# First feed-forward entry on ACT and DVE, and own SBUF tiles for the up weights of one chunk per stage

## The chip, the cores and the metric

The kernel runs on one core of one Trainium2 chip. The time is the device time of one execution, in microseconds (us), and a kernel's time is the median of its runs. TensorE is called PE here, VectorE DVE, ScalarE ACT, GpSimd POOL and SyncE SP; `PEld` in a profile is TensorE's weight load.

## The reference

Two small models run one after the other on a sequence of 256 rows of width 1024. The first is a hybrid attention layer with a mixture of 32 experts. The second has two layers, each with a SwiGLU feed-forward before and behind its mixer, so four feed-forward stages in all, and they are where the change lies:

```python
def swiglu(x, w_gate, w_up, w_down):
    return (jax.nn.silu(x @ w_gate) * (x @ w_up)) @ w_down

def second_block(x, ...):
    h = x                                  # rms_norm of the first model's result
    for layer in range(DEPTH_2):           # 2
        h = h + 0.5 * swiglu(rms_norm_2(h, norm_ffn[layer, 0]), ...)
        hn = rms_norm_2(h, norm_mix[layer])
        h = h + (pool_fox_mixer(hn, ...) if layer % 2 == 0 else mla_mixer(hn, ...))
        h = h + 0.5 * swiglu(rms_norm_2(h, norm_ffn[layer, 1]), ...)
    return rms_norm_2(h, norm_final)
```

The width inside a feed-forward is 2816, and all is float32.

## The kernel before

Every large product is made in three matmuls. A float32 operand is split into a high part H, rounded to the matmul's fp32r type, and the remainder L; the product is H·XH + H·XL + L·XH. `split` (L191 on) does it: ACT writes H (L195, or L199 where a column scale goes in), DVE writes L (L196, L200). The argument `late` puts the L half on another engine. Weights come by DMA from SP's queue into the pool `raw` (6 buffers, L205) and are split into the ring `hl` (8 buffers), in two halves of 128x1024 each (`load_split`, L203).

`ffn(n, g0)` is one feed-forward stage, n = 0 to 3. It walks over 11 chunks of 256 inner columns. A chunk has a gate group (48 matmuls of 128x256 into a PSUM bank `ps`), an up group (48, bank `psq`), and, one chunk later, a down group (48, into four banks `psa`). `project` and `ws` emit them; the first gate group goes by contraction rows instead (`ws_by_k`), so that it can start on the first inputs. Between these groups TensorE's stream holds the small float32 matmuls that make the norm's factor: `add_sums` adds squares over partitions, `rsqrt_of` works out the reciprocal root in small steps (L218 to L224 on DVE, L219 to L229 on POOL), and `row` spreads it over the partitions: it makes two diagonal tiles `dg` (L268 on DVE, L270 on POOL) and multiplies them with a block of ones, two fp32 matmuls (four records in a trace) into `psa` beside or within the second chunk's up group. In the first stage a second `row` follows later (`later`, in the third chunk's `act`).

A list scheduler sets the order on each engine from the program's data dependences; `tc.issue_after(i)` holds what is emitted inside it behind instruction i. Tiles of one pool take turns by tag.

The entry of the first stage follows the last expert pair. `spread` (L984 on, the callables in `due`) multiplies the experts' outputs back into token order, 2 of 8 blocks of `xT` at a time, and DVE adds them into `xT` (L993). The blocks are split into `first_x`, the first stage's input XH and XL, scaled by the columns `gg`. The squares for two sums follow (`squares`, L244 to L253). The first gate weights are split by ACT (H) and by POOL (L, through `late=(G, G)`); the `dg` tiles of the first stage's first `row` are made by POOL too.

The input tiles come from the pool `x8`, the weights from `hl`; both are float32r, 8 KB per partition. In the built program the ring's weights begin at byte 608 modulo 1024 of a partition (96 for their second 128 columns), the input at 32.

At the end, the result goes out in four DMAs, two from ACT's queue and two from SP's (L1527).

Of the kernel before, what the change touches and what calls it, by code (L numbers as in the profile page):

```python
# [10 lines left out]
F32 = mybir.dt.float32  # L11
F32R = mybir.dt.float32r
# [86 lines left out]
def tile_hybrid(ctx: ExitStack, tc: tile.TileContext, d: dict, out: bass.AP, stop=None, dbg=None):  # L99
# [22 lines left out]
    def nm(s):  # L122
        n_names[0] += 1
        return f"{s}_{n_names[0]}"
# [10 lines left out]
    def raw(shape):  # L135
        return raw_p.tile(shape, F32, tag="raw", name=nm("raw"))

    def hl(shape, dt=F32R):
        return hl_p.tile(shape, dt, tag="hl", name=nm("hl"))

    def x8(dt=F32, shape=(128, KD, T)):
        return x8_p.tile(list(shape), dt, tag="x8", name=nm("x8"))
# [48 lines left out]
    def split(src, H, L, scale=None, late=None):  # L191
        if scale is None:
            n = src.shape[1] // 2 if src.shape[1] > 1 and len(src.shape) == 3 and src.shape[1] * src.shape[2] == 2048 else src.shape[1]
            for c in range(0, src.shape[1], n):
                A.activation(H[:, c:c + n], src[:, c:c + n], AF.Copy)  # L195
                (late[c > 0] if late else V).tensor_tensor(L[:, c:c + n], src[:, c:c + n], H[:, c:c + n].bitcast(F32),  # L196
                                                          op=OP.subtract)
        else:
            a = A.activation(H, src, AF.Copy, scale=scale)  # L199
            v = V.scalar_tensor_tensor(L, src, scale, H.bitcast(F32), op0=OP.mult, op1=OP.subtract)  # L200
            return [a.ins, v.ins]

    def load_split(src_ap, shape, late=None):  # L203
        r = raw(shape)
        SP.dma_start(r, src_ap)  # L205
        H, L = hl(shape), hl(shape)
        split(r, H, L, late=late)
        return H, L

# [107 lines left out]
    def pview(a, n):  # L317
        return a.rearrange("p (k f) -> p k f", k=n)
# [197 lines left out]
    po = ps()  # L516
# [469 lines left out]
    def spread(y, GT, b):  # L986
        po = ps()
        for j in (2 * b, 2 * b + 1):
            for n in range(2):
                last = mm(po[:, (j % 2) * T:(j % 2 + 1) * T], y[j // 4][n][:, (j % 4) * 128:(j % 4 + 1) * 128], GT,  # L990
                          n == 0 and j % 2 == 0, n == 1, skip_group_check=True)
        for j in (2 * b, 2 * b + 1):
            V.scalar_tensor_tensor(xT[:, j, :], po[:, (j % 2) * T:(j % 2 + 1) * T], g2c[:, j:j + 1], xT[:, j, :],  # L993
                                   op0=OP.mult, op1=OP.add)
        return last

    pin, due = [], []

    def behind_one(i):
        return tc.issue_after(i) if i is not None else ExitStack()  # L1000
# [47 lines left out]
    for p in range(NEXP // 2):  # L1048
# [13 lines left out]
        if p == 13:  # L1062
            overflow()

    first_x += [x8(F32R), x8(F32R)]
    for b in range(4):
        due.pop(0)()
        for j in (2 * b, 2 * b + 1):
            pins[:] = split(xT[:, j, :], first_x[0][:, j, :], first_x[1][:, j, :], scale=gg[:, j:j + 1])

    pm.close()
    pe.close()
# [61 lines left out]
    def ffn(n, g0, done=None):  # L1134
# [2 lines left out]
        XHL, narrow, *later = prep("nffn", g0) if n else prep_first(pf)  # L1137
        acc4 = []

        def wf(w, c, nk, late=None):  # L1140
            o = (3 * c + w) * 2048
            return load_split(pview(d["wf"][n, :, o:o + 2048], nk), [128, nk, 2048 // nk], late)

        def down(c, aHL, HL):
            first, last = c == 0, c == FC - 1
# [37 lines left out]
        for c in range(FC):  # L1183
            with ExitStack() as es:
                if n + c == 0:
                    for i in pin[-2:]:
                        es.enter_context(tc.issue_after(i))
                if c == 1:
                    es.enter_context(after(pins[1:]))
                HLg = wf(0, c, KD, (G, G) if n + c == 0 else None)  # L1190
                if c == 0:
                    HLu = wf(1, c, KD)
            pg = ps()
            last = project(HLg, pg) if c else ws_by_k(pg, HLg, XHL)
            if c == 1:
                with tc.issue_after(last):
                    r = row(*rn)
                act(*held, r)
            if c:
                with tc.issue_after(shifted[-1] if n else ended[0]) if c == 1 else ExitStack():  # L1200
                    HLu = wf(1, c, KD)
            elif n:
                rn = narrow(last)
            pu = psq()
            last = project(HLu, pu)
            if n + c == 0:
                rn = narrow(last)
            if not c:
                acc4 += [psa() for _ in range(4)]
                held = (c, pg, pu)  # L1210
                continue
            act(c, pg, pu, r)
# [309 lines left out]
    for i in range(2):  # L1522
        A.activation(gained[i], gained[i], AF.Copy, scale=r[:, i:i + 1])
        o = po_.tile([128, 512], F32, name=nm("o"))
        V.scalar_tensor_tensor(o, bank[2 * i + 1], r[:, i:i + 1], nfb[:, 512:], op0=OP.mult, op1=OP.mult)
        for q, (t, E) in enumerate(((gained[i], A), (o, SP))):
            E.dma_start(out[i * 128:(i + 1) * 128, q * 512:(q + 1) * 512], t)  # L1527


def lay_out(i):  # L1530
# [66 lines left out]
```

## Time and profile before

| | us |
|---|---|
| three runs | 1654.90, 1649.27, 1648.03 |
| median | 1649.27 |
| profiled execution, its own time | 1654.91 |
| its span in the trace | 1653.1 |
| first stage, first gate group to last down group | 694.5 to 888 |
| second stage, middle | 1016.8 to 1169 |
| third stage, middle | 1192.8 to 1362.4 |
| fourth stage, middle | 1475.1 to 1636 |

The profile is one execution, recorded by the hardware; its time lies at the upper end of the three runs. A row of a timeline puts neighbouring instructions of one kind together: start, time from the first's start to the last's end, engine, line, operation, output<-inputs, shape, count, and in brackets the idle time before it with what ended it. The chain of waits goes back from the last instruction, at each step to what released it. [...]

### The profile page before, as it was taken

To read this page: it belongs to the slowest core of one execution; us is meant where nothing else is said; L and a number is where in the kernel's file an instruction comes from. 1 tells how busy PE (TensorE), PEld (TensorE's weight loads), DVE (VectorE), ACT (ScalarE), POOL (GpSimd) and SP (SyncE) were. 2 spreads that over 40 slices of the span, in tenths; PEclk is the share of its full clock that TensorE was granted. 3 is DMA by queue.
4 is the path that set the end of the run, shared out by engine and by line. 5 is a ranking of instruction groups with operands and counts; after the bars stand their busy time and mean duration, and the time that the engine had idled before them with its cause. 6 is when DMAs were issued, how large, how long until landed. Compare 5 with 4: busy or idle time off the path is not lost.

```text
span 1653.1 us, 26911 instructions
## 1 busy us (share of the span) xinstructions
PE 1577.7 (95%) x11239; PEld 1248.5 (76%) x11239; DVE 926.0 (56%) x1670; ACT 579.2 (35%) x883; POOL 158.3 (10%) x270
## 2 busy tenths in 40 slices
PE   5988989999999999899999999999999999999997
PEld 2867853344434443499999899999999998899997
DVE  4587545325434423576557557556755567575554
ACT  2444420000000000343444554444544355554342
POOL 0796000000000000110002101000100002010000
PEclk9998999999999999999999999999999999999998
DMA  9763799999999999965555325655555543165520
GB/s 379 312 209 129 258 371 366 412 421 420 421 420 421 421 421 416 388 212 179 184 191 194 103 102 204 204 184 199 182 199 181 182 153 128 64 224 185 181 100 26
DMA packets 62252, 411.11 MB, mean 249 GB/s; under 512 B 6704, under 2 KB 8752, under 8 KB 15920
## 3 DMA queue, kind: packets, MB, share of 16 engines
q1 hardware_dynamic: 61840, 408.85, 65.4%
q8 instruction: 89, 1.46, 0.4%
q10 hardware_dynamic: 288, 0.52, 0.1%
q14 instruction: 35, 0.29, 0.0%
HBM read 408.30 MB, written 1.05 MB: 248 GB/s over the span
## 4 chain that ended last, share of the span: by engine, by line
PE 53%; DVE 4%; DMA 2%; POOL 1%; issue 1%; ACT 0%; DVEq 0%; SPq 0%; ACTq 0%; POOLq 0%
PE psa L149 20%; PE psq L149 16%; PE ps L149 16%; DMA we<-in_we_dram 1%; DVE hl L196 1%; DVE x L200 1%; DMA hl<-in_we_dram 1%; PE psa L459 1%; DVE xT L1155 0%; POOL rt L227 0%; POOL rt L228 0%; POOL ry L219 0%; DVE sq L251 0%; POOL rt L226 0%; POOL ry L229 0%
## 5 line engine op out<-in xcount | busy, mean ns | idle before, releaser
L195 ACT ACTIVATE hl<-raw 128x1024 fp32r<-128x1024 f32 (+1 forms) x338 | 346.9, 1060 | 404.7 <-issue 252.1
L196 DVE TENSOR_TENSOR hl<-raw,hl 128x1024 fp32r<-128x1024 f32 (+1 forms) x336 | 412.2, 1243 | 120.8 <-ACT hl L195 120.5
L149 PE MATMUL ps<-x,hl 128*128 128x256 f32 x3120 | 391.6, 284 | 6.1 <-ACT hl L195 2.7
L149 PEld LDWEIGHTS ps<-x,hl 128*128 128x128 f32 x3120 | 375.1, 190 | 20.8 <-issue 7.2
L149 PE MATMUL psq<-x,hl 128*128 128x256 f32 x2160 | 262.4, 281 | 1.3 <-ACT hl L195 1.3
L149 PEld LDWEIGHTS psq<-x,hl 128*128 128x128 f32 x2160 | 256.9, 190 | 1.5 <-ACT hl L195 1.5
L149 PE MATMUL psa<-aH,hl 128*128 128x256 f32 x1408 | 253.8, 280 | 0.0
L149 PEld LDWEIGHTS psa<-aH,hl 128*128 128x128 f32 x1408 | 217.9, 188 | 0.0
L149 PE MATMUL psa<-aL,hl 128*128 128x256 f32 x704 | 196.9, 280 | 0.1
L149 PEld LDWEIGHTS psa<-aL,hl 128*128 128x128 f32 x704 | 133.6, 190 | 0.4 <-DVE aL L196 0.3
L149 PE MATMUL psa<-hl,XT 128*64 128x512 f32 x464 | 120.8, 599 | 1.4 <-DMA hl<-in_we_dram 1.4
L1040 ACT ACTIVATE ym<-psa,gs 128x512 fp32r<-128x512 f32 x32 | 21.9, 687 | 248.6 <-PE psa L149 243.7
L149 PE MATMUL psa<-raw,XT 128*64 128x512 f32 x368 | 100.4, 598 | 1.4 <-DVEq L862 1.1
L993 DVE SCALAR_TENSOR_TENSOR xT<-ps,mod,xT 128x256 f32<-128x256 f32 x128 | 55.7, 479 | 77.8 <-PE ps L149 77.6
L149 PEld LDWEIGHTS psa<-hl,XT 128*64 128x64 f32 x464 | 34.8, 136 | 55.0 <-issue 46.7
L1164 DVE TENSOR_TENSOR gr<-ps,row 128x512 f32<-128x512 f32 x44 | 30.4, 690 | 80.3 <-PE ps L149 80.3
L1041 DVE SCALAR_TENSOR_TENSOR ym<-psa,gs,ym 128x512 fp32r<-128x512 f32 x32 | 24.0, 750 | 88.1 <-ACT ym L1040 86.4
L149 PEld LDWEIGHTS ps<-GT,ym 128*128 128x128 f32 x256 | 34.2, 188 | 50.2 <-issue 36.6
L1166 DVE TENSOR_TENSOR ur<-psq,row 128x512 f32<-128x512 f32 x44 | 30.4, 691 | 71.2 <-PE psq L149 71.2
L1018 ACT ACTIVATE ac<-psa 128x512 f32<-128x512 f32 x16 | 9.6, 597 | 166.5 <-PE psa L149 140.4
L149 PE MATMUL psa<-hl,aT 128*64 128x512 f32 x240 | 63.4, 615 | 0.3 <-DVE aT L1030 0.2
L1022 DVE TENSOR_TENSOR ac<-ac,psa 128x256 f32<-128x256 f32 x32 | 12.1, 417 | 91.2 <-PE psa L149 91.2
(363 smaller groups left out, 1751.1 us busy)
## 6 DMA issues: line engine op xcount, KB each, us to landing
raw<-in_wf_dram SPq DMA_DIRECT2D x132, 1024.0 KB, 4.9
hl<-in_we_dram SPq DMA_DIRECT2D x88, 1024.0 KB, 18.3
raw<-in_we_dram SPq DMA_DIRECT2D x68, 1024.0 KB, 19.8
raw<-in_ada_dram SPq DMA_DIRECT2D x24, 1024.0 KB, 7.8
we<-in_we_dram SPq DMA_DIRECT2D x23, 1024.0 KB, 18.4
wmw<-in_we_dram SPq DMA_DIRECT2D x11, 1024.0 KB, 17.7
raw<-in_w_in_dram SPq DMA_DIRECT2D x10, 1024.0 KB, 7.3
raw<-in_ab_in_dram SPq DMA_DIRECT2D x8, 1024.0 KB, 4.9
```

Of the source, the lines that this page charges most:

```text
L149: return getattr(PE.matmul(o, l, r, start=start, stop=stop, **kw), "ins", None)
L195: A.activation(H[:, c:c + n], src[:, c:c + n], AF.Copy)
L196: (late[c > 0] if late else V).tensor_tensor(L[:, c:c + n], src[:, c:c + n], H[:, c:c + n].bitcast(F32), op=OP.subtract)
L200: v = V.scalar_tensor_tensor(L, src, scale, H.bitcast(F32), op0=OP.mult, op1=OP.subtract)
L459: PE.transpose(bk[:, n * 128:(n + 1) * 128], P[:, n * 128:(n + 1) * 128], ident)
L993: V.scalar_tensor_tensor(xT[:, j, :], po[:, (j % 2) * T:(j % 2 + 1) * T], g2c[:, j:j + 1], xT[:, j, :], op0=OP.mult, op1=OP.add)
L1018: A.activation(ac, p1, AF.Silu)
L1022: V.tensor_tensor(ac[:, c], ac[:, c], p3[:, c], op=OP.mult)
L1040: last = A.activation(H, py[n], AF.Copy, scale=gs).ins
L1041: V.scalar_tensor_tensor(L, py[n], gs, H.bitcast(F32), op0=OP.mult, op1=OP.subtract)
L1164: V.tensor_tensor(gr, v2(pg), b2(r), op=OP.mult)
L1166: V.tensor_tensor(ur, v2(pu), b2(r), op=OP.mult)
```

## The change

It has three parts. First, the first gate weights are loaded ahead, in the loop that ends the experts, and split there by ACT and DVE alone, one half between each of the first two pairs of sums and the `x` splits that follow; the order of sums, weight halves and `x` splits is written out by `issue_after`. The first `row` makes its `dg` tiles on DVE. Second, the up weights of the second chunk of every stage, and of the fourth chunk of the first stage, go into two tiles of their own, `zH` and `zL`, in the stage's pool `wf`, instead of the ring `hl`. In the built program `zH` and `zL` begin at 32 modulo 1024 (544 for the second 128 columns), so at the place of the input. Third, the four output DMAs all go out from SP's queue.

```diff
-    def load_split(src_ap, shape, late=None):
+    def load_split(src_ap, shape, late=None, own=None):
         r = raw(shape)
         SP.dma_start(r, src_ap)
-        H, L = hl(shape), hl(shape)
+        H, L = own or (hl(shape), hl(shape))
         split(r, H, L, late=late)
         return H, L
...
-            V.scalar_tensor_tensor(xT[:, j, :], po[:, (j % 2) * T:(j % 2 + 1) * T], g2c[:, j:j + 1], xT[:, j, :],
-                                   op0=OP.mult, op1=OP.add)
+            summed[:] = [V.scalar_tensor_tensor(xT[:, j, :], po[:, (j % 2) * T:(j % 2 + 1) * T], g2c[:, j:j + 1], xT[:, j, :],
+                                                op0=OP.mult, op1=OP.add).ins]
...
     first_x += [x8(F32R), x8(F32R)]
+    r = raw([128, KD, 256])
+    SP.dma_start(r, pview(d["wf"][0, :, :2048], KD))
+    first_w = hl([128, KD, 256]), hl([128, KD, 256])
+    done = None
     for b in range(4):
-        due.pop(0)()
+        with behind_one(done):
+            due.pop(0)()
+        done = summed[0]
+        if b < 2:
+            c = slice(4 * b, 4 * b + 4)
+            with tc.issue_after(pin[-1]):
+                A.activation(first_w[0][:, c], r[:, c], AF.Copy)
+            with tc.issue_after(done):
+                done = V.tensor_tensor(first_w[1][:, c], r[:, c], first_w[0][:, c].bitcast(F32), op=OP.subtract).ins
         for j in (2 * b, 2 * b + 1):
-            pins[:] = split(xT[:, j, :], first_x[0][:, j, :], first_x[1][:, j, :], scale=gg[:, j:j + 1])
+            with tc.issue_after(done):
+                pins[:] = split(xT[:, j, :], first_x[0][:, j, :], first_x[1][:, j, :], scale=gg[:, j:j + 1])
+            done = pins[1]
...
+        def own(c):
+
+            if c == 1 or not n and c == 3:
+                return [pf.tile([128, KD, 256], F32R, tag=t, name=nm(t), bufs=1) for t in ("zH", "zL")]
...
                 if n + c == 0:
-                    for i in pin[-2:]:
-                        es.enter_context(tc.issue_after(i))
+                    es.enter_context(after(pins))
...
-                HLg = wf(0, c, KD, (G, G) if n + c == 0 else None)
+                HLg = wf(0, c, KD) if n + c else first_w
...
-                    r = row(*rn)
+                    r = row(*rn, eng=None if n else V)
...
-                    HLu = wf(1, c, KD)
+                    HLu = wf(1, c, KD, own(c))
...
-        for q, (t, E) in enumerate(((gained[i], A), (o, SP))):
-            E.dma_start(out[i * 128:(i + 1) * 128, q * 512:(q + 1) * 512], t)
+        for q, t in enumerate((gained[i], o)):
+            SP.dma_start(out[i * 128:(i + 1) * 128, q * 512:(q + 1) * 512], t)
```

**DVE at the end of the experts.** What follows the last expert's L1041, before; `x_961` and `x_962` are the first input's H and L, `ps_...` the banks of the sums:

```order
L993 SCALAR_TENSOR_TENSOR xT<-ps_5084,mod,xT 128x256 x2
L993 SCALAR_TENSOR_TENSOR xT<-ps_5095,mod,xT 128x256 x2
L200 SCALAR_TENSOR_TENSOR x_962_5083<-xT,gg,x_961_5082 128x256 x4
L993 SCALAR_TENSOR_TENSOR xT<-ps_5106,mod,xT 128x256 x2
L993 SCALAR_TENSOR_TENSOR xT<-ps_5117,mod,xT 128x256 x2
```

And with the change (`hl_5087` is the first gate weights' L, `sq_5250` the running squares):

```order
L993 SCALAR_TENSOR_TENSOR xT<-ps_5088,mod,xT 128x256 x2
L1080 TENSOR_TENSOR hl_5087<-raw_5084,hl_5086 128x1024
L200 SCALAR_TENSOR_TENSOR x_962_5083<-xT,gg,x_961_5082 128x256 x2
L993 SCALAR_TENSOR_TENSOR xT<-ps_5101,mod,xT 128x256 x2
L1080 TENSOR_TENSOR hl_5087<-raw_5084,hl_5086 128x1024
L200 SCALAR_TENSOR_TENSOR x_962_5083<-xT,gg,x_961_5082 128x256 x2
L993 SCALAR_TENSOR_TENSOR xT<-ps_5114,mod,xT 128x256 x2
L251 TENSOR_TENSOR sq_5250<-sq_5250,sq_5253 128x512
L200 SCALAR_TENSOR_TENSOR x_962_5083<-xT,gg,x_961_5082 128x256 x2
L993 SCALAR_TENSOR_TENSOR xT<-ps_5125,mod,xT 128x256 x2
```

Two weight halves and one addition of squares now stand between the sums.

**ACT at the same place.** Before (`hl_5136` are the first gate weights, `hl_5144` the first up weights):

```order
L195 ACTIVATE hl_5136<-raw_5134 128x1024 x2
L199 ACTIVATE x_961_5082<-xT,gg 128x256 x4
L195 ACTIVATE hl_5144<-raw_5142 128x1024 x2
L199 ACTIVATE x_961_5082<-xT,gg 128x256 x4
L247 ACTIVATE sq_5250<-xT,cols 128x256 x2
```

With the change, from the addition for the second sum (`acc_5266`) on:

```order
L244 ACTIVATE acc_5266<-xT 128x512
L195 ACTIVATE zH_5385<-raw_5387 128x1024
L199 ACTIVATE x_961_5082<-xT,gg 128x256 x2
L247 ACTIVATE sq_5257<-xT,cols 128x256 x2
L195 ACTIVATE zH_5385<-raw_5387 128x1024
L199 ACTIVATE x_961_5082<-xT,gg 128x256 x2
L195 ACTIVATE hl_5144<-raw_5142 128x1024 x2
```

The second chunk's up weights (`zH`) now stand ahead of the last four inputs, and the first up weights behind them.

**DVE ahead of the first stage's first row.** Before, the small steps of `rsqrt_of` follow one another, and `dg` is POOL's:

```order
L1114 SCALAR_TENSOR_TENSOR rv_5249<-rw_5133,rv_5249 128x2
L218 TENSOR_SCALAR ri_5285<-rv_5249 128x2
L218 TENSOR_SCALAR ri_5632<-rw_5133 128x2
L219 TENSOR_SCALAR ry_5286<-ri_5285 128x2
L222 SCALAR_TENSOR_TENSOR rt_5287<-ry_5286 128x2
```

With the change (`hl_5503` and `hl_5511` are the first two down weights, `hl_5568` the third chunk's up weights; four rows at the cut are small steps as before):

```order
L1129 SCALAR_TENSOR_TENSOR rv_5249<-rw_5141,rv_5249 128x2
L196 TENSOR_TENSOR hl_5503<-raw_5500,hl_5502 128x1024
L218 TENSOR_SCALAR ri_5285<-rv_5249 128x2
...
L196 TENSOR_TENSOR hl_5511<-raw_5508,hl_5510 128x1024
L222 SCALAR_TENSOR_TENSOR rt_5287<-ry_5286 128x2
...
L196 TENSOR_TENSOR hl_5568<-raw_5565,hl_5567 128x1024
L224 SCALAR_TENSOR_TENSOR ry_5286<-rt_5287,ry_5286 128x2
...
L196 TENSOR_TENSOR zL_5386<-raw_5387,zH_5385 128x1024
L268 TENSOR_SCALAR dg_5360<-cstt,ry_5286 128x128 x2
```

The small steps stand between weight halves, and `dg` comes behind them and the first half of `zL`. On PE, three matmuls of the up group that reads `zH` and `zL` stand ahead of the two of `row`, where none stood before; the third of them is the first that reads `zL`.

## Rows read from the trace of the kernel before

**Rows 1.** The page's first part: busy us, share of the span, instructions.

```profile
PE 1577.7 (95%) x11239; PEld 1248.5 (76%) x11239; DVE 926.0 (56%) x1670; ACT 579.2 (35%) x883; POOL 158.3 (10%) x270
```

**Rows 2.** Windows, PE's matmuls of L149: us, busy (count), PEclk, DMA share, GB/s.

```profile
741.30:888.00 146.70, 146.70 (x1248) 1.00 0.55 186
1016.80:1169.00 152.20, 152.20 (x1345) 1.00 0.57 193
1192.80:1362.40 169.60, 169.60 (x1442) 1.00 0.54 181
1475.10:1636.00 160.90, 160.90 (x1369) 1.00 0.41 138
```

**Rows 3.** Chain of waits in the first and third stage: start us, us, what.

```profile
735.64 5.88 PE psq L149 x52
741.52 5.66 PE psa L149 x48
...
1181.39 5.44 PE ps L149 x48
...
1186.83 0.47 PE psa L149 x4
1187.30 5.66 PE psq L149 x48
1192.95 5.76 PE psa L149 x48
```

**Rows 4.** Timeline of PE at the first stage's entry, columns as told above.

```profile
694.53 7.33 PE L149 MATMUL ps<-x,hl 128*128 128x256 f32 x48 [2.54 <-DVE xT L993]
...
716.84 0.84 PE L149 MATMUL psa<-dg,cstt 128*128 128x128 f32 x4 [3.10 <-POOL dg L270]
717.43 7.32 PE L149 MATMUL psq<-x,hl 128*128 128x256 f32 x48
724.60 0.62 PE L149 MATMUL psa<-aH,hl 128*128 128x256 f32 x4
```

**Rows 5.** Window behind that wait: us, busy of PE, PEld, DVE, ACT, POOL, PEclk, DMA, GB/s.

```profile
719.00:721.00 2.00, 2.00 (x11) 2.00 (x11) 2.00 (x5) 0.63 (x1) 0.52 (x1) 0.50 0.23 90
```

**Rows 6.** Timeline of PE in the experts, a gather.

```profile
617.86 2.14 PE L149 MATMUL ps<-Gt,x 128*128 128x256 f32 x16
```

**Rows 7.** Timeline of POOL at the entry.

```profile
687.74 4.87 POOL L196 TENSOR_TENSOR hl<-raw,hl 128x1024 fp32r<-128x1024 f32 x2 [487.46 <-PE ps L149]
```

**Rows 8.** Timeline of DVE at the entry.

```profile
687.42 1.65 DVE L993 SCALAR_TENSOR_TENSOR xT<-ps,mod,xT 128x256 f32<-128x256 f32 x4
689.04 4.65 DVE L200 SCALAR_TENSOR_TENSOR x<-xT,gg,x 128x256 fp32r<-128x256 f32 x4
...
695.18 1.66 DVE L200 SCALAR_TENSOR_TENSOR x<-xT,gg,x 128x256 fp32r<-128x256 f32 x4
...
700.43 1.22 DVE L196 TENSOR_TENSOR hl<-raw,hl 128x1024 fp32r<-128x1024 f32 x1
...
702.17 0.69 DVE L251 TENSOR_TENSOR acc<-acc,sq 128x512 f32<-128x512 f32 x1
...
712.22 0.16 DVE L224 SCALAR_TENSOR_TENSOR ry<-rt,ry 128x2 f32<-128x2 f32 x1
```

**Rows 9.** Groups by line and shape, DVE's `dg`: busy us, mean ns, idle before.

```profile
L268 DVE TENSOR_SCALAR dg<-cstt,ry 128x128 f32<-128x128 f32 x8 | 2.4, 338 | 0.1
```

**Rows 10.** Timeline of SP's queue: the fourth and fifth weight load of the stage.

```profile
680.65 0.82 SPq L205 DMA_DIRECT2D raw<-in_wf_dram  x2
```

**Rows 11.** DMA issues of 681.0 to 681.5: count, size, median us to landing.

```profile
raw<-in_wf_dram SPq DMA_DIRECT2D x1, 1024.0 KB, 13.7
```

**Rows 12.** Timeline of ACT at the entry.

```profile
686.62 1.99 ACT L195 ACTIVATE hl<-raw 128x1024 fp32r<-128x1024 f32 x2
688.51 1.70 ACT L199 ACTIVATE x<-xT,gg 128x256 fp32r<-128x256 f32 x4
```

**Rows 13.** Timeline of SP's queue at the end.

```profile
1647.77 0.94 SPq L1527 DMA_DIRECT2D out_dram<-o  x2
```

More of the change, by code (lines that the diff above doesn't have):

```diff
@@ L992, in spread @@
         for j in (2 * b, 2 * b + 1):
-            V.scalar_tensor_tensor(xT[:, j, :], po[:, (j % 2) * T:(j % 2 + 1) * T], g2c[:, j:j + 1], xT[:, j, :],
-                                   op0=OP.mult, op1=OP.add)
+            summed[:] = [V.scalar_tensor_tensor(xT[:, j, :], po[:, (j % 2) * T:(j % 2 + 1) * T], g2c[:, j:j + 1], xT[:, j, :],
+                                                op0=OP.mult, op1=OP.add).ins]
         return last
-    pin, due = [], []
+    pin, due, summed = [], [], []
     def behind_one(i):
@@ L1138, in ffn, with wf @@
         acc4 = []
-        def wf(w, c, nk, late=None):
+        def wf(w, c, nk, own=None):
             o = (3 * c + w) * 2048
-            return load_split(pview(d["wf"][n, :, o:o + 2048], nk), [128, nk, 2048 // nk], late)
+            return load_split(pview(d["wf"][n, :, o:o + 2048], nk), [128, nk, 2048 // nk], None, own)
+        def own(c):
+            if c == 1 or not n and c == 3:
+                return [pf.tile([128, KD, 256], F32R, tag=t, name=nm(t), bufs=1) for t in ("zH", "zL")]
         def down(c, aHL, HL):
```

## The prediction

> **What bounds the kernel now.** First the page: PE is busy 95% of the span and no other engine comes near it [rows 1]. So I read how fast TensorE's stream runs, stage by stage, before any wait. Over the long middle of each of the four feed-forward stages PE is busy all the time, at granted clock 1.00, and still the stages differ: 146.70 us for 1248 matmuls in the first, 152.20 for 1345 in the second, 169.60 for 1442 in the third, 160.90 for 1369 in the fourth [rows 2]. That is 117.5, 113.2, 117.6 and 117.5 ns each, for the same shape, the same order and the same clock. The chain says it plainer, since nearly all of it is groups of 48 matmuls: a group takes 5.44 us or 5.65, and a stage stays with one of the two [rows 3]. I call them the quick and the slow pace; a group differs by 0.21.
>
> The next thing to see is where the pace turns. The third stage begins quick (48 in 5.44 at 1181.4). Then come the four records of the small fp32 matmuls that `row` puts into the stream, and from the next group on it is slow, 5.66, 5.76, then 5.65 to its end. The first stage turns in the same place: 5.88 for 52 that include the second `row`, then 5.66. The second is quick after its `row`, the fourth slow [rows 2, 3]. So an interruption can leave either pace, and a stage keeps what it got. That is all the trace shows; it doesn't show what makes a pace.
>
> Last, the entry of the first stage, 685 to 741 us. Here PE does wait: the first gate group of 48 begins at 694.53 and takes 7.33, the second chunk's up group begins at 717.43 behind the `row` records of 716.84 and takes 7.32, and the down group follows at 724.60 [rows 4]. [...]
>
> **Part one: the placement.** In the built programs the weights (`hl`) begin at 608 and, for the second 128 columns, at 96 modulo 1024 bytes of a partition; the input begins at 32. For five groups (one per stage, two in the first) the new tiles put the weights at 32 and 544. Each of the five is the first or third group behind a `row`. Work doesn't change: same matmuls, and the splits of these weights go the same way over ACT and DVE. What it can change is the pace of these five groups and, because a pace lasts, that of the rest of the stage.
>
> The trace of before has no fp32r matmul with weights and input at the same place. Nearest are the quick and slow group (5.44, 5.76 at most in a stretch without a wait [rows 3]); further off is the gather of the experts, with weights at 32 and 544 and moving rows at 352, 16 in 2.14 us, which makes 6.4 for 48 [rows 6]. So the five groups cost between -1.0 (as much below the quick pace as the slow one is above it; no row is below 5.44) and +4.8. I take 5.65, the nearest: +1.0.
>
> What they leave behind decides the case. 48 matmuls under another address relation are a far longer disturbance than the four records that turn the pace now, and the same one in every stage, so I expect the same result in each: all quick or all slow. I take quick as the likelier, because the quick pace is what the trace shows directly after most waits (at 1181.39 [rows 3], and through the whole second stage). Then the first stage gains 23 groups (741 to 888 is 26; two run before the fourth chunk's up group, and that is the third), the third stage 30 (1192.95 to 1362.4), the fourth 28 (1475 to 1636): 81 x 0.21 = -17.2 us. The second is quick already.
>
> **Part two: the entry without GpSimd.** Gone: GpSimd's split of the first gate weights (4.87 for two halves), beside which four `x` splits on DVE took 4.65 instead of 1.66 [rows 7, 8]. That is 3.0 us on the path to 694.53. But the order puts other work there. On DVE now: two sums into `xT` (0.41 each), a weight half (1.2), two `x` splits (0.41 each) [rows 8], again all that, then the third pair of sums, which frees the PSUM bank of the first gate group. From 687.42: 0.82 + 1.2 + 0.82, twice, + 0.82 = 693.9. So the start gains 0.6, not 3.0.
>
> Then ACT. The first half of the new `zH` stands ahead of the inputs 4 to 7. It is the fifth weight load, the second of two issued from 680.65 on, at 681.1; one issued there takes 13.7 to land, so it is there at 694.8 [rows 10, 11]. ACT then needs zH 1.0, two inputs 0.85, two squares (taken at an input's 0.43 each) 0.85, zH 1.0, two inputs 0.85 [rows 12]: 699.3. DVE's last input is ready at 699.8, the first group ends by 700.8 (now 701.9, 694.53 + 7.33 [rows 4]), and the first up group, whose weights come behind that on ACT and DVE (700.3, 701.5), ends at 706.8. Behind these halves DVE has four additions of squares (0.69), two of half that width (0.4) and two weight halves (1.22) [rows 8], 6.0, and waits for ACT's squares, say 0.6: the second sum of squares ends at 708.1, and the second gate group, whose turn comes behind the small matmuls that read it, runs from there, 44 x 0.115, to 713.5.
>
> DVE's queue is now the path. Between the sums and `dg` stand seven weight halves, the last two being the third chunk's up weights, whose buffer is free when the second gate group ends: 713.5 + 2.1 for two ACT halves + 1.2 = 716.8; DVE's own queue from 708.1 (seven halves of 1.15, eight small steps of 0.16, 0.2 with their issue [rows 8]) comes to 717.6. I take 718.2, both with their latencies. Seven small steps of 0.2 follow, 1.4; the first half of `zL`, 1.2; `dg`, two of 0.34 [rows 9]: 721.4. The third matmul of the second up group reads `zL`, so PE stands from 713.7 to 720.8, and the `row` records follow at 721.4. They end at 722.0; then 45 matmuls at 0.113 and the 1.7 that the lower clock adds to this group now (717.43 to 724.60 is 7.2, for 5.44 [rows 4]), 5.1 + 1.7: 728.8 against 724.60. **The entry costs 4.2 us**, since the wait for GpSimd's `dg` is gone and one for DVE's longer queue is there. From both sides: 1.0 if the gate group starts at the full clock (1.3 less) and the halves are as short as 1.13; 6.0 if ACT and DVE wait on each other once more in each pair.
>
> **Part three: the end.** The four stores go out from one queue instead of two by two from 1647.7 on [rows 13]. A store takes that queue 0.35 to 0.5, so the last is issued 0.5 later: +0.5 (0 to 1).
>
> **The sum.** The profiled execution took 1654.9: -17.2 + 1.0 + 4.2 + 0.5 = -11.5, so 1643.4. The other two runs of before are 5.6 and 6.9 below it, about what one stage at the other pace is worth (30 x 0.21 = 6.3). If that is what they are, quick stages bring all runs to 1643; if the profiled run is merely 6 longer, to 1637. I take the middle, **1640 us**.
>
> **The rivals.**
> Placement does nothing. [...] The trace neither shows nor excludes it: pace changes there come with interruptions, at one placement. In this kernel it would mean that `row` decides as now, and only entry and end count: 1649.3 + 4.7 = 1654.0, within 0.5%.
>
> The five groups leave the slow pace (the other side). Then the second stage loses its 30 groups (+6.3), the first another three (+0.6), and entry, end and the groups' own time cost 5.7: 1654.9 + 12.6 = 1667.5, slower than before. It decides from the point where the group behind the second stage's up group takes 5.65. For it: two of the three groups that follow a `row` directly in stages two to four run slow now. Against it: the second stage, with the same order, doesn't.
>
> Each stage falls as it likes. Half of 111 groups (81 slow now, 30 quick) slow: -81 x 0.105 + 30 x 0.105 = -5.4, + 5.7: about 1650 to 1655, by which run of before one starts from.
>
> **How the numbers follow.** Quick everywhere 0.56, with 1634 to 1647; no effect 0.22 (1650 to 1656); slow everywhere 0.12 (1660 to 1670); mixed 0.10 (1644 to 1656). The range 1634 to 1656 leaves out the slow case and the edges. About 0.5%, 8.2 us, is what a measurement of this kernel can tell from no change, so faster means below 1641.0: some 0.68 of the first case and 0.3 of the mixed one, 0.42. Slower means above 1657.5: the slow case and what is left of the others' upper ends, 0.19. The rest, 0.39, is same.
>
> **What would show it.** In the chain of the changed kernel: 5.44 from the group behind each of the five up groups to the stage's end, and 5.44 to 5.8 for the five themselves. 5.65 in the second stage would be the slow case; a pace that differs between stages, with the turn still at `row`, no effect. In the entry: the second up group's third matmul waits some 7 us for DVE's `zL`, and the first down group starts near 729; if it starts before 724.6, my reading of DVE's queue is wrong. If the five groups take over 6.4 each, my bound for them is.

## The result and the profile after

The changed kernel takes 1676.59 us, the median of four runs from 1676.21 to 1677.48. The kernel before took 1649.98 in the runs beside it (1648.03 to 1654.90). The ratio is 1.0158, interval 1.0127 to 1.0189: slower, by 27 us between the medians. The forecast was 1640 with a range from 1634 to 1656.

The profiled execution took 1676.21 against 1654.91. The first part of its page (busy time, share and instructions of each engine), beside [rows 1], shows PE with the same 11239 matmuls, and busy with them 11 us longer:

```profile
PE 1588.9 (95%) x11239; PEld 1258.1 (75%) x11239; DVE 924.9 (55%) x1674; ACT 578.2 (35%) x883; POOL 161.5 (10%) x266
```

So the first view to read is again the pace by stage. These are windows inside the four stages, matmuls of L149 alone, columns as in [rows 2] (PEclk is the granted clock, as a share of full speed):

```profile
751.50:888.00 136.50, 136.50 (x1160) 1.00 0.53 179
1024.00:1169.00 145.00, 145.00 (x1233) 1.00 0.54 182
1216.00:1362.40 146.40, 146.40 (x1246) 1.00 0.54 181
1508.10:1636.00 127.90, 127.90 (x1088) 1.00 0.45 155
```

That is 117.5 to 117.7 ns a matmul in the four, the slow pace. The second stage, 113.2 in [rows 2], is slow too now. The chain of waits shows where it begins. These are the end of the entry and the second stage's beginning (start us, us, what), to be read beside [rows 3, 4]:

```profile
720.24 0.58 PE psq L149
720.82 0.85 PE psa L149 x4
721.67 6.75 PE psq L149 x45
728.42 5.65 PE psa L149 x48
...
1011.60 0.84 PE psa L149 x4
1012.44 5.75 PE psq L149 x48
1018.20 5.65 PE psa L149 x48
1023.85 5.65 PE ps L149 x48
```

At 1012.44 stands the group whose weights lie at the input's place. It takes 5.75, and everything behind it 5.65.

The second thing to see is the rows that come late. The timeline of POOL has the first small step of each `row`, and the timeline of DVE what runs beside it in the second stage:

```profile
999.94 7.82 POOL L219 TENSOR_SCALAR ry<-ri 128x2 int32<-128x2 int32 x1 [56.38 <-DVE ri L218]
...
1190.50 7.83 POOL L219 TENSOR_SCALAR ry<-ri 128x2 int32<-128x2 int32 x1 [178.60 <-DVE ri L218]
...
1478.18 6.76 POOL L219 TENSOR_SCALAR ry<-ri 128x2 int32<-128x2 int32 x1 [76.52 <-DVE ri L218]
```

```profile
999.60 0.17 DVE L218 TENSOR_SCALAR ri<-rv 128x2 int32<-128x2 int32 x1
999.67 1.23 DVE L196 TENSOR_TENSOR hl<-raw,hl 128x1024 fp32r<-128x1024 f32 x1
1000.80 2.36 DVE L196 TENSOR_TENSOR zL<-raw,zH 128x1024 fp32r<-128x1024 f32 x2
1003.08 4.63 DVE L196 TENSOR_TENSOR hl<-raw,hl 128x1024 fp32r<-128x1024 f32 x4
```

A step on two numbers per partition, 0.20 elsewhere, takes 7.82 and ends at 1007.76. DVE's seven weight halves end at 1007.71. In the kernel before the same step took 3.28 beside three halves (995.26 for 3.50), and it ended at 998.80, where they ended at 998.76. The same two views of the kernel before, in the second stage and then in the third:

```profile
995.52 3.28 POOL L219 TENSOR_SCALAR ry<-ri 128x2 int32<-128x2 int32 x1 [56.37 <-DVE ri L218]
...
995.26 3.50 DVE L196 TENSOR_TENSOR hl<-raw,hl 128x1024 fp32r<-128x1024 f32 x3
...
1178.84 1.03 POOL L219 TENSOR_SCALAR ry<-ri 128x2 int32<-128x2 int32 x1 [174.12 <-DVE ri L218]
...
1178.59 2.36 DVE L196 TENSOR_TENSOR hl<-raw,hl 128x1024 fp32r<-128x1024 f32 x2
```

In the second stage of both kernels POOL's step ends when DVE's unbroken run does, and the run is now four halves longer. The reading is that the ring holds DVE back less, because two of its buffers came free; that the own tiles lengthen the run, e2_entry_only and e3_own_only show below. That the step ends with the run is no rule: in the third stage of before it ended at 1179.87, 0.05 behind the first of two halves (1179.81), and the second followed without a gap. Why POOL got its turn there isn't shown. The timeline of PE shows what the late step costs in the changed kernel:

```profile
1011.60 0.84 PE L149 MATMUL psa<-dg,cstt 128*128 128x128 f32 x4 [1.96 <-POOL dg L270]
...
1202.17 1.15 PE L149 MATMUL psa<-dg,cstt 128*128 128x128 f32 x4 [2.23 <-POOL dg L270]
...
1488.79 1.09 PE L149 MATMUL psa<-dg,cstt 128*128 128x128 f32 x4 [3.10 <-POOL dg L270]
```

Set against the same places of the kernel before, the 21.3 us between the two profiled executions are:

| where | us |
|---|---|
| entry, to the first down group (728.25 in the timeline, for 724.60 [rows 4]; the chain, which sets a start behind the modelled end of the matmul before, has 728.42) | 3.7 |
| first stage: three groups that were quick before (0.6), the fourth chunk's own group (0.1) | 0.7 |
| second stage: row late, slower group behind it | 2.6 |
| second stage's slow pace, up to the third stage's row: 31 groups (6.5), less 0.4 for shorter waits | 6.1 |
| third stage: row late (2.4), lower clock in the group behind (0.52 from 1204 to 1206, 1.00 behind that; 6.94 for 5.66 [rows 3]) and in the row (0.63 from 1202 to 1204) | 4.2 |
| fourth stage: row late (2.8), the same (0.50 from 1490 to 1492; 6.89) | 4.2 |
| end | -0.2 |

The medians lie further apart, 26.6, since the profiled execution of before was one of its slowest, and the runs of the changed kernel all lie within 1.3 us.

### The profile page after: what moved, and what is told of

Read it like the earlier page. It is cut to its first block, busy times and chain, and to the rows that moved or that the text cites. A ratio compares the mean times of both kernels' runs of the same rounds, so it can differ in the third digit from the quotient of the medians.

```text
span 1674.4 us, 26902 instructions
## 1 busy us (share of the span) xinstructions
PE 1588.9 (95%) x11239; PEld 1258.1 (75%) x11239; DVE 924.9 (55%) x1674; ACT 578.2 (35%) x883; POOL 161.5 (10%) x266
## 4 chain that ended last, share of the span: by engine, by line
PE 69%; DMA 15%; POOL 8%; DVE 5%; issue 1%; ACT 1%; SPq 0%; DVEq 0%; POOLq 0%; ACTq 0%
PE psa L149 31%; PE ps L149 20%; PE psq L149 16%; DMA hl<-in_we_dram 6%; DMA raw<-in_we_dram 5%; POOL acc L584 3%; POOL tap L583 3%; DMA we<-in_we_dram 2%; POOL ry L219 1%; DVE hl L196 1%; DMA raw<-in_wf_dram 1%; DMA raw<-in_ada_dram 1%; PE psa L459 1%; ACT x L199 0%; PE psq L1029 0%
## 5 line engine op out<-in xcount | busy, mean ns | idle before, releaser
L195 ACT ACTIVATE hl<-raw 128x1024 fp32r<-128x1024 f32 (+1 forms) x326 | 334.3, 1060 | 405.7 <-issue 243.7
L196 DVE TENSOR_TENSOR hl<-raw,hl 128x1024 fp32r<-128x1024 f32 (+1 forms) x326 | 400.0, 1244 | 126.1 <-ACT hl L195 125.9
L149 PE MATMUL ps<-x,hl 128*128 128x256 f32 x3120 | 393.0, 284 | 5.0 <-ACT hl L195 2.7
L149 PEld LDWEIGHTS ps<-x,hl 128*128 128x128 f32 x3120 | 376.6, 190 | 19.7 <-issue 7.2
L149 PE MATMUL psa<-aH,hl 128*128 128x256 f32 x1408 | 256.2, 281 | 0.0
L149 PE MATMUL psq<-x,hl 128*128 128x256 f32 x1920 | 233.6, 281 | 0.3 <-DVE hl L196 0.3
L149 PEld LDWEIGHTS psq<-x,hl 128*128 128x128 f32 x1920 | 228.9, 189 | 0.5 <-DVE hl L196 0.5
L149 PEld LDWEIGHTS psa<-aH,hl 128*128 128x128 f32 x1408 | 220.3, 190 | 0.0
L149 PE MATMUL psa<-aL,hl 128*128 128x256 f32 x704 | 197.5, 281 | 0.0
L149 PEld LDWEIGHTS psa<-aL,hl 128*128 128x128 f32 x704 | 132.2, 188 | 0.0
L219 POOL TENSOR_SCALAR ry<-ri 128x2 int32<-128x2 int32 (+1 forms) x7 | 23.8, 3393 | 1024.3 <-DVE rt L223 518.3
L149 PE MATMUL psa<-hl,XT 128*64 128x512 f32 x464 | 120.4, 599 | 0.3 <-DMA hl<-in_we_dram 0.3
L149 PE MATMUL psa<-raw,XT 128*64 128x512 f32 x368 | 101.9, 607 | 1.4 <-DVEq L862 1.1
L149 PEld LDWEIGHTS psa<-hl,XT 128*64 128x64 f32 x464 | 35.0, 136 | 53.3 <-issue 46.5
L149 PEld LDWEIGHTS ps<-GT,ym 128*128 128x128 f32 x256 | 34.5, 190 | 52.2 <-issue 39.1
L1041 DVE SCALAR_TENSOR_TENSOR ym<-psa,gs,ym 128x512 fp32r<-128x512 f32 x32 | 24.0, 751 | 86.6 <-ACT ym L1040 84.9
L149 PEld LDWEIGHTS psa<-raw,XT 128*64 128x64 f32 x368 | 29.4, 139 | 47.3 <-issue 41.2
```

Source lines behind the costliest of these rows:

```text
L149: return getattr(PE.matmul(o, l, r, start=start, stop=stop, **kw), "ins", None)
L219: E.tensor_scalar(y.bitcast(I32), iv, -1.0, 1597463007.0, op0=OP.mult, op1=OP.add)
L1041: V.scalar_tensor_tensor(L, py[n], gs, H.bitcast(F32), op0=OP.mult, op1=OP.subtract)
```

## The experiments

Three theories stood at the start. The **queue theory**: the extra buffers let DVE run ahead, and the late rows and the entry's loss come from that. The **place theory**: a group's distance between weights and input sets the pace that the stage then keeps, and distance 0 leaves the slow one. The **chance theory**: a pace falls anew at each interruption, and the place has nothing to do with it. "Distance" is weights minus input modulo 512 bytes, so that both 128-column halves of a group have the same; the ring's is 64.

To compare paces across kernels, matmuls are counted in the same four stretches of each profiled execution (770 to 870, 1040 to 1150, 1220 to 1330, 1500 to 1600 us), one in each stage. Quick is 885, 973, 973, 885; slow is 852, 937, 937, 852.

| kernel | 1st | 2nd | 3rd | 4th | median us | ratio to before (interval) |
|---|---|---|---|---|---|---|
| before | 852 | 973 | 937 | 852 | 1649.98 | |
| changed | 851 | 936 | 937 | 851 | 1676.59 | 1.0158 (1.0127 to 1.0189) |
| e1_own_ring_place | 851 | 973 | 936 | 885 | 1663.03 | 1.0054 (1.0024 to 1.0083) |
| e2_entry_only | 851 | 973 | 937 | 885 | 1643.46 | 0.9951 (0.9928 to 0.9974) |
| e3_own_only | 851 | 973 | 936 | 851 | 1678.60 | 1.0181 (1.0141 to 1.0222) |
| e5_hold | 852 | 973 | 973 | 885 | 1654.99 | 0.9995 (0.9972 to 1.0018) |
| e6_own128 | 885 | 973 | 973 | 885 | 1656.25 | 1.0035 (1.0006 to 1.0064) |
| b1_reset128 | 885 | 973 | 973 | 884 | 1637.57 | 0.9909 (0.9877 to 0.9942) |
| b1_same_chip | 885 | 973 | 973 | 885 | 1637.26 | 0.9889 (0.9872 to 0.9907) |
| b4_reset0 | 852 | 937 | 936 | 851 | 1656.32 | 1.0021 (1.0001 to 1.0042) |
| b2_ring320 | 851 | 973 | 936 | 852 | 1650.89 | 0.9967 (0.9950 to 0.9983) |
| b3_ring448 | 852 | 936 | 936 | 852 | 1660.93 | 1.0024 (1.0011 to 1.0038) |

The kernel before was measured beside each group of runs, on several chips: 1651.69 (19 runs, 1642.9 to 1661.6) beside e1 to e3, 1656.38 (23 runs) beside b1_reset128, b2, b3 and e5, 1653.58 (18 runs) beside b1_same_chip, b4 and e6. Its runs spread over 20 us. By an estimate from the traces, 26 to 31 groups a stage at 0.21, four stages that can each be 6 us slower or not give about that.

### The parts apart

**Without tiles of their own** (all up weights in the ring, the rest as changed):

```diff
-                    HLu = wf(1, c, KD, own(c))
+                    HLu = wf(1, c, KD)
```

> The changed kernel without tiles of their own: all up weights lie in the ring again, the new entry and the stores from one queue stay. Queue theory: DVE's small steps stand together again and dg comes behind one weight half, POOL L219 takes 3.5 us or less in the second and third stage, no wait for the row is there; the first down group starts at 718 to 721, 4 to 7 us earlier than before. Rival (the new entry itself costs the 3.8 us): first down group at 727 or later. Time by the queue theory with paces as before 1644 to 1651, by the rival 1653 to 1660.

The entry falls within the queue theory's range, and the time, 1643.46, just below the 1644 to 1651 that it gave. The chain of waits there:

```profile
713.62 0.35 PE psq L149 x3
713.98 0.45 PE psa L149 x4
714.42 5.30 PE psq L149 x45
719.72 0.23 PE ps L149 x2
719.96 2.11 PE psa L149 x17
```

The `row` follows the up group's third matmul without a wait, and the down group starts at 719.96 in the chain and 719.79 in the timeline, 4.8 us earlier than before and 8.5 earlier than in the changed kernel. POOL's step is back at 3.28 in the second stage. So the new entry by itself is a gain, and the 3.7 us that it lost in the changed kernel belong to the own tiles, whose weight halves stood between DVE's small steps and `dg`.

**Only the own tiles**, on the kernel before, old entry:

```diff
-                    HLu = wf(1, c, KD)
+                    HLu = wf(1, c, KD, own=own(c))
```

> The kernel before with one difference: the tiles of their own, at the input's place, for the second chunk's up weights of each stage and the fourth's of the first. Queue theory: POOL L219 takes 7 to 8 us in the second, third and fourth stage, and some 10 us are lost to rows that come late; in the entry dg is POOL's and comes behind DVE's longer queue too. Placement theory: all stages at 5.65 behind these groups. Both together 1668 to 1676. If the new entry was what made POOL's step long, it takes 3.3 us at most here and the time is below 1660.

POOL's step in the second stage is as long as in the changed kernel, with the old entry around it:

```profile
1001.33 7.82 POOL L219 TENSOR_SCALAR ry<-ri 128x2 int32<-128x2 int32 x1 [56.28 <-DVE ri L218]
```

The time, 1678.6, lies 2.6 us above the range that was expected. Another thing was not expected: the profiled execution (1672.04, the quickest of its four runs) has the second stage quick (973), although a group at distance 0 stands there. Its chain of waits there, with that group at 1013.86:

```profile
1013.02 0.84 PE psa L149 x4
1013.86 7.26 PE psq L149 x48
1021.12 5.44 PE psa L149 x48
```

The group stands behind a late row. Its first pairs of matmuls took 0.60 to 0.63 and its later ones 0.40, as in the third stage of the changed kernel, where pairs of 0.63 stand at granted clock 0.52 and pairs of 0.40 at 1.00; so I take it to have begun at the lower clock. It took 7.26, and no wait lies between it and the quick group behind it. In the changed kernel the groups of the third and fourth stage began at the lower clock as well (0.52 and 0.50; 6.94 and 6.89) and left the slow pace. So a group that the clock's rise falls into doesn't always leave the same pace; the undisturbed one at 1012.44 in the changed kernel left the slow one.

**The own tiles at the ring's place** (a pad of 576 bytes ahead of them, 608 modulo 1024):

```diff
+                pf.tile([128, 144], F32, tag="zpad", name=nm("zpad"), bufs=1)
                 return [pf.tile([128, KD, 256], F32R, tag=t, name=nm(t), bufs=1) for t in ("zH", "zL")]
```

> The changed kernel with one difference: the tiles of their own lie at 608 modulo 1024, the place of the ring's weights, and no longer at the input's. Queue theory (two more buffers let DVE run six or seven weight halves without a break, and POOL's first small step of the row waits for the end of that run): nothing changes in it, POOL L219 again takes 7 to 8 us in the second, third and fourth stage, and the row is late there by some 2, 4 and 4 us; the entry is as in the changed kernel, first down group at 728.4. Placement theory (the groups at the input's place leave the slow pace): the five groups then run like any other, and at least the second stage goes back to 5.44 us a group, -6.3 us: about 1670. Chance theory (a stage's pace falls anew at every interruption, whatever the place): stages differ from one execution to another, and the runs spread over 6 us or more below 1677.

POOL's L219 takes 7.82, 7.83 and 6.76, and the first down group starts at 728.2: the queue's part is untouched. The paces are mixed again, two quick stages in the profile, and the runs spread from 1652 to 1665, below all runs of the changed kernel. The median is 1663.0, where the place theory gave some 1670 for the second stage alone; in the profile the fourth is quick too. So buffers and place are two separate losses. The spread is what the chance theory expected as well; what speaks against that one comes below.

**DVE's run cut short.** In the second to fourth stage two of DVE's loads make their L halves only behind the copy of the row (L273):

```diff
+                held_by[:] = copied if n and not c else []
                 prev.append((c, (aH, aL), wf(2, c, 2)))
+                held_by[:] = []
...
+                held_by[:] = copied if n and c == 2 else []
                 HLg = wf(0, c, KD) if n + c else first_w
+                held_by[:] = []
```

> The changed kernel with one difference: in the second to fourth stage DVE makes the L halves of the first chunk's down weights and of the third chunk's gate weights only behind the copy of the row. Queue theory: two halves instead of seven stand ahead of POOL's first small step, L219 takes 2 to 3 us, the row of the second and third stage is in time again and that of the fourth comes 4 to 5 us earlier; the stages stay slow behind the groups at the input's place: 1676.6 - 2.1 - 2.4 - 4.9, about 1667. If POOL's wait has another cause, L219 stays at 7 to 8 us and the time at 1676.

The small step is short (L224 is this kernel's L219):

```profile
997.18 1.02 POOL L224 TENSOR_SCALAR ry<-ri 128x2 int32<-128x2 int32 x1 [55.38 <-DVE ri L223]
```

It takes 1.02 in the second and the third stage, 1.09 in the fourth, and the rows of all three stages come without a wait for `dg`. So a shorter run of DVE does make the rows timely, as forecast. Two sizes are not as forecast. The step takes 1.02 where 2 to 3 were expected. And the time is 22 us less than the changed kernel's, where 9.4 were expected, on a chip where the kernel before was 6 slower. The held halves make PE wait 0.2 us for `aL` just behind the group at distance 0, and the stage turns quick there; the third and the fourth stage have the same wait (0.22 and 0.21) and turn in the same place. That is the profiled execution, the quickest of ten; the others took up to 1663.28 and have no trace. The timeline of PE has the wait, the chain what follows:

```profile
1015.27 0.38 PE L149 MATMUL psa<-aL,hl 128*128 128x256 f32 x1 [0.22 <-DVE aL L201]
```

```profile
1020.52 5.21 PE ps L149 x46
1025.74 5.44 PE psq L149 x48
```

So this run settles the cause of the late rows, but its time mixes two effects.

### What sets the pace

**Eleven distances in one kernel.** On the kernel before, the up weights of the chunks 3, 5, 7 and 9 go into a tile of their own, each time at another distance. No `row` and no wait stands beside these groups. It ran once, in 1646.55 us:

```diff
+        PROBE = ({3: 0, 5: 128, 7: 256, 9: 384}, {3: 0, 5: 192, 7: 320, 9: 448},
+                 {3: 32, 5: 96, 7: 224, 9: 64}, {3: 0, 5: 128, 7: 256, 9: 384})
...
-                    HLu = wf(1, c, KD)
+                    HLu = wf(1, c, KD, own=own(c))
```

> The kernel before with a tile of its own for the up weights of the chunks 3, 5, 7 and 9 of every stage, each time at another distance from the input modulo 512 bytes (first and fourth stage 0, 128, 256, 384; second 0, 192, 320, 448; third 32, 96, 224 and 64, which is the ring's own distance). These groups stand between other groups, with no interruption beside them. Placement theory: a group at distance 0 takes 5.75, and what follows it is slow (5.65) even where the stage was quick; another distance may leave 5.44. Chance theory: the stage goes on at the pace that it had, whatever the place; only the groups themselves differ.

The chain of the second stage, from a quick stretch over a group at distance 0 (1035.86) to one at 192 (1069.89) and one at 320 (1102.74):

```profile
1030.42 5.44 PE ps L149 x48
1035.86 5.76 PE psq L149 x48
1041.62 5.65 PE psa L149 x48
...
1069.89 5.65 PE psq L149 x48
1075.54 5.44 PE psa L149 x48
...
1102.74 5.44 PE psq L149 x48
1108.18 5.44 PE psa L149 x48
```

All sixteen groups:

| distance | the group itself, us | pace ahead to pace behind |
|---|---|---|
| 0 | 5.76 | slow to slow, quick to slow twice |
| 256 | 5.76 | quick to slow twice |
| 128 | 5.70 | slow to quick twice |
| 384 | 5.70 | slow to quick twice |
| 192 | 5.65 | slow to quick |
| 32, 96, 224 | 5.68, 5.76, 5.60 | quick to quick |
| 64, 320, 448 | 5.44 | quick to quick |

The chance theory falls for undisturbed groups: the pace turns right at these groups, at no interruption, and each distance that came more than once did the same each time. The place theory holds, with the sign against the forecast: distance 0, which the change chose, leaves the slow pace. What a stage gets at a `row` or behind a wait is not settled by this run.

**One group per stage, 128 against 0.** On the kernel of e2_entry_only the fourth chunk's up weights of every stage get their own tile, at distance 128 (b1) or 0 (b4). The two kernels differ by one offset:

```diff
+            if c == 3:
+                z = pf.tile([128, 4128], F32R, tag="z", name=nm("z"), bufs=1)
+                return [z[:, o:o + 2048].rearrange("p (k c) -> p k c", c=256) for o in (32, 2080)]   # b1
+                                                                                 for o in (0, 2048)]    # b4
```

> The kernel of e2_entry_only with one difference: the fourth chunk's up weights of every stage lie in a tile of their own, 128 bytes from the input's place modulo 512 (160 and 672 modulo 1024). Place theory (what a group with another distance leaves behind, the stage keeps; p1 showed 128 leave the quick pace twice where the stage was slow): every stage is at 5.44 from the fourth chunk's down group on, whatever it was ahead; two slow stages of e2 gain 22 groups of 0.21 each, the reset group costs 0.05 to 0.26: about 1635, and the runs lie closer together than those of e2. Chance theory: 1643 and paces as they fall. Queue theory: the tile stands behind the row and costs nothing there, POOL L219 as in e2.

> The kernel of b1_reset128 once more, on the chip of b4_reset0, so that the two differ by the distance of one group per stage alone. Place theory: every stage at 5.44 from the fourth chunk's down group on, 1635 to 1638. Chance theory: as b4_reset0.

> The kernel of b1_reset128 with one difference: the fourth chunk's tile lies at the input's place modulo 512 (distance 0), no longer 128 bytes from it. Place theory: a group at distance 0 leaves 5.65 behind it, so all four stages are slow from the fourth chunk's down group on: 88 groups of 0.21 more, 18 us, so about 1655. Chance theory: no difference from b1.

In both, the second stage came to that group slow. The chain of b1_same_chip, then of b4_reset0:

```profile
1025.73 5.66 PE ps L149 x48
1031.39 5.70 PE psq L149 x48
1037.09 5.45 PE psa L149 x48
```

```profile
1028.60 5.65 PE ps L149 x48
1034.26 5.76 PE psq L149 x48
1040.02 5.65 PE psa L149 x48
```

All four stages quick with 128, all four slow with 0, on the same chip 1637.26 against 1656.32: 19.1 us, where 18 were expected. b1 is also the quickest kernel of this study, 1.1 per cent below the kernel before and 0.9 per cent in its first measurement. Its first four runs were 1635.0 to 1637.9 with one at 1646.7, which has no trace; why it was longer is open.

**The changed kernel with its tiles moved by 128 bytes:**

```diff
+                pf.tile([128, 32], F32, tag="zpad", name=nm("zpad"), bufs=1)
                 return [pf.tile([128, KD, 256], F32R, tag=t, name=nm(t), bufs=1) for t in ("zH", "zL")]
```

> The changed kernel with one difference: its own tiles lie 128 bytes further on, at 160 and 672 modulo 1024. Place theory: the five groups then leave the quick pace; stages one to four at 5.44 unless a wait or a second row behind the group throws the pace anew: 70 to 105 groups of 0.21 less, 1655 to 1662. Queue theory: L219 still takes 7 to 8 us and the first down group still starts near 728, since the tiles are as many as before. Chance theory: spread as in e1_own_ring_place, around 1663.

The windows of its four stages:

```profile
770.00:870.00 100.00, 100.00 (x885) 1.00 0.56 192
1040.00:1150.00 110.00, 110.00 (x973) 1.00 0.57 192
1220.00:1330.00 110.00, 110.00 (x973) 1.00 0.57 193
1500.00:1600.00 100.00, 100.00 (x885) 1.00 0.53 179
```

All are quick, POOL's step is as long as ever (7.83 in the second stage), and the entry's stop for `zL` is there too:

```profile
719.65 0.58 PE L149 MATMUL psq<-x,zL 128*128 128x256 f32 x1 [5.48 <-DVE zL L196]
```

The median is 1656.25, 20 us below the changed kernel. Its runs spread over 17 us, 1650.7 to 1668.0. Its groups stand behind late rows, as those of e3_own_only do, so probably not every execution gets the pace that an undisturbed group would leave; only one execution has a trace, so this isn't shown. This is the nearest thing to undoing the place alone, and it shows both halves: by the medians the place cost some 20 us, and with it mended the own tiles still leave the kernel no quicker than before. The other half has a size too: b1_same_chip, on the same chip, is quick in all four stages as well, has its own tile in the fourth chunk only, and its profiled execution is 15.0 us shorter (1638.98 against 1654.00).

**The whole ring at another distance.** The gap between ring and input is made 256 or 384 bytes smaller, on e2_entry_only:

```diff
-    gap(448)
+    gap(192)    # b2: distance 320
+    gap(64)     # b3: distance 448
```

> The kernel of e2_entry_only with the gap between ring and input 256 bytes smaller: every group of every stage, gate, up and down, has its weights 320 bytes from the input modulo 512 and no longer 64. In p1 a group at 320 in a quick stage took 5.44. If the distance decides which paces there are, and 320 has the quick one alone: all four stages at 5.44 throughout, about 1632. If 320 has a slow pace of its own too: stages differ again, 1638 to 1655. The same by chance theory.

> As b2_ring320, with the gap 384 bytes smaller than in e2_entry_only, which makes the distance 448 modulo 512. In p1 a group at 448 in a quick stage took 5.44. Quick pace alone: about 1632; a slow pace of its own: 1638 to 1655.

No gain: with 320 both paces occur, as with 64 (one quick stage of four in the profile), with 448 all four stages are slow, and the median, 1660.93, lies above the 1638 to 1655 expected. So a distance that left a quick stage quick, once, is not one that has the quick pace alone. A single group in an undisturbed stretch turned slow stages quick, at 128 in p1_places and b1_same_chip (5.70 itself, 5.46 and 5.45 behind it) and at 192 and 384 in p1_places; the whole ring at 128 was not run.

## Why the prediction was wrong

**What bounds the kernel.** The reading held: two paces, 5.44 and 5.65, kept by a stage, and TensorE's stream as the path.

**The entry** was worked out as 4.2 and measured 3.7. Its steps came within 0.6 us: first gate group 693.9 (694.22), the stop for `zL` to 720.8 (720.24), `dg` 721.4 (720.82 in the chain), first down group 728.8 (728.25 in the timeline). The experiment adds what the sum didn't say: without the own tiles this entry gains 4.8, so all of its loss comes with the halves that the own tiles let in, PE's stop behind them (5.61) and the lower clock behind the stop. That clock was 0.50 from 720 to 724 in the changed kernel, as it was from 719 to 721 in the kernel before [rows 5]; the 45 matmuls behind the `row` took 6.75, where 5.1 and 1.7 were summed.

**The five groups themselves**: +1.0 was taken, 5.65 each; undisturbed ones took 5.75, which against the slow pace that they had before is 0.1 each.

**The step that failed** is "I take quick as the likelier". That the same result would stand in every stage was right; which one was put on a pace seen behind waits, not on any group at that distance. The term of -17.2 (81 groups at 0.21 are 17.0) became +6.7 (second stage's pace 6.1, three groups of the first 0.6). The trace of before had no such group, and with the sign unknown the honest weight was nearer even than 0.56 to 0.12. The rival "the five groups leave the slow pace" named the mechanism and its price, 1667.5 from the profiled execution of before; that of the changed kernel took 1676.2.

**The missing term** is 11.0 us: second to fourth stage, rows that come late and slower groups right behind them. The sum put it at nothing. "The splits of these weights go the same way over ACT and DVE" is true of the work and not of the times. I costed the longer queue of DVE at the entry and did not look at the other three stages, where DVE now makes 7, 7 and 6 weight halves between its last small step (L218) and the row's copy, for 5, 4 and 4 before, and where the trace of before showed POOL's step in the second stage ending 0.04 us behind DVE's run. The trace of the changed kernel has 7.82 us for a step that takes 0.20 alone: it ended 0.05 behind the last of seven DVE instructions in a row, while in the third stage of before it took 1.03 and ended behind the first of two. What holds POOL's step meanwhile isn't shown.

**The end**: +0.5 was taken, about 0.2 was there from the last DVE instruction to the span's end (5.6 against 5.4); the table's -0.2 holds 0.4 that the last steps ahead of it took less.

**Placement does nothing** falls as well: entered at the quick pace in p1_places, groups take 5.44 to 5.76 by the distance alone, at granted clock 1.00. Why the distance counts isn't shown.

What stays open is what a pace is inside TensorE, which pace a `row` leaves, why a wait of 0.2 us behind a group at distance 0 was followed by the quick pace (e5_hold), and what a group leaves when the clock rises within it (e3_own_only against the changed kernel). The runs show what turns an undisturbed stretch, not how.

## What to carry to other kernels

Where a stream of equal matmuls has more than one pace, find out what turns it by moving one group inside an undisturbed stretch, and read the group behind it; then place one such group per stretch, away from waits. A buffer that is added is a change of order on the engine that fills it: list what that engine now runs ahead of each small step that another engine waits for, in every stage and not only in the one that was edited. And where single runs spread by as much as one stage's pace, one profiled execution is one throw: compare medians of many.

## What the runs showed of the hardware

- fp32r matmuls of 128x256 ran at 113.3 or 117.7 ns each over whole groups of 48 (5.44 or 5.65 us) and at 113.3 to 120 in the sixteen groups of p1_places (5.44 to 5.76), all at granted clock 1.00, by the distance in SBUF between weights and moving rows and by what ran ahead. At one distance (64) both paces persist: in the kernel before 113.2 ns over 152.20 us and 117.6 over 169.60 [rows 2].
- In b1_same_chip the second stage came slow (5.66) to one group of 48 at distance 128, which took 5.70, and left it quick (5.44); all four stages are quick in their windows (885, 973, 973, 885). With that group at 0, in b4_reset0, the second stage came slow and stayed so (5.65, the group 5.76, then 5.65), and all four are slow (852, 937, 936, 851). In p1_places a group at 0 that was entered at 5.44 took 5.76 and left 5.65 behind it.
- Beside seven back-to-back weight halves on DVE (8.0 us) a GpSimd instruction on 128x2 numbers took 7.82 us in the changed kernel and ended 0.05 us behind them; in e5_hold, which holds part of these halves back, it took 1.02. In the third stage of the kernel before such an instruction took 1.03 and ended 0.05 us behind the first of two halves.
- In e5_hold three stages turned quick right behind a wait of 0.2 us (0.22, 0.22 and 0.21) in the group that follows one at distance 0. Two matmuls of the next gate group stand ahead of that wait, and no run had the wait alone.
